# Smaller weight tiles, stores issued by ScalarE, and one threshold search in a decoder layer on one core

## The chip, the core and the metric

The kernel runs on one core of a Trainium2 chip. The core has TensorE (PE, matrix products; its weight loads are PEld), VectorE (DVE), ScalarE (ACT), GpSimd (POOL) and SyncE (SP), which here only issues DMAs. Each engine works through its own instructions in their order; semaphores hold an instruction until what it needs is done. The metric is the device time of one execution in microseconds (us).

## The reference: what is computed

One decoder layer for a sequence of 1024 tokens of width 1024, all in float32. One projection of x yields the inputs of two kinds of heads. Eight attention heads of 64 see, per query, only the 256 keys that an indexer scores highest. Four HGRN2 heads of 128 run a gated recurrence. Then come an output projection, a layer norm, an MLP and a second layer norm:

```python
proj = x @ w_in[l]
q, k, v, iq, ik, iw, hq, hf, hi, hg = jnp.split(proj, _split_points(), axis=-1)
...
score = jnp.einsum('bqh,bqhs->bqs', iwb.astype(jnp.float32), jax.nn.relu(logits))
...
_, idx = lax.top_k(score, topk)
...
mix = jnp.concatenate([att, hgo], axis=-1) @ w_o[l]
x = layer_norm(ALPHA * x + mix, ln1_g[l], ln1_b[l])
h = jnp.square(jax.nn.relu(x @ w_up[l])) @ w_down[l]
x = layer_norm(ALPHA * x + h, ln2_g[l], ln2_b[l])
```

## The kernel before

Every float32 matrix is split into a high part (rounded by ACT, line 88) and a low part (the remainder, by DVE or POOL, line 89). A product is then three matmuls (`mm3`, lines 123 to 125). For projection weights POOL makes the low part.

A tile scheduler sets the order of each engine's instructions when the kernel is built, from the program's order and modelled times. On the chip that order is fixed. Rotating buffers (`bufs`) decide how early a load can be issued: it waits until the previous user of its buffer is done.

The first 464 us, the stage that most of the change touches, are:

- 0 to 42 us: x is loaded and transposed, and the indexer's columns are projected.
- Then `turned` projects keys and queries. A pass (two PSUM banks, 48 matmuls) is followed by rope on DVE (lines 191 and 192) and POOL (193), by a split into `rparts`, and by four stores of 256 KB to DRAM (`kd`, `qd`). These DMAs are issued by SP at line 49. Between the passes stand the indexer's logits: matmuls at 282 and 283, `relu` on ACT at 286, weighted sums into six `score` tiles on DVE at 288 and 290.
- Then `natural`, `transposed` and `gates` project the recurrence's inner input (`HI`, copied by ACT at 430), its queries and gates (`hgq`, `hgf`), attention's values (`vd`, stored at line 561) and the output gates.
- Beside these stand two generators. `hgrn` is the recurrence: a unit per head, with 32x32 block products at line 482 and DVE work at 486 to 542 (`hgD` at 502 copies blocks out of PSUM). The other is the search for each query's 256th best score.

The search sets one bit of a threshold after the other, 31 in all. Four score tiles are counted by DVE (`topk_counts`): `cand` at 325 proposes a bit, four `reach` operations at 313 count scores (384 to 768 wide), `acc` at 328 and a copy at 329 keep or drop it. Two wider tiles are counted by ACT (`topk_signs`): sums of signs, `sjunk` at 345, with three small DVE operations per bit: `scand` 355, `sacc` 357, `scur` 358. `select` (381 to 388) then turns each score tile into a mask; attention's first scores, at line 691 from 464 us on, need the masks.

The weights of a projection live in `wraw` (2 buffers) and `w` (5 buffers) as tiles of two blocks of 128 rows, so that a tile of 512 columns is 512 KB to load. The table `side` says how many steps of each generator are taken beside each projection step:

Of the kernel before, what the change touches and what calls it, by code (L numbers as in the profile page):

```python
# [7 lines left out]
F32 = mybir.dt.float32  # L8
# [34 lines left out]
def layer(ctx, tc, x, w_in, w_o, lb_logits, hg_norm_g, ln1_g, ln1_b, w_up, w_down, ln2_g, ln2_b,  # L43
# [54 lines left out]
    def weight(srcs, shape, pool_every=2, after=None, halves=False, pool=None):  # L98

        raw = (pool or wp).tile([P] + shape, F32, name="wraw", tag="wraw", bufs=4 if pool else 2)  # L100
# [8 lines left out]
        w = wp.tile([P, 2] + shape, F32R, name="w", tag="w", bufs=5)  # L109
# [45 lines left out]
    def in_weights(segs, pool_every=1, pool=None):  # L155
        n = sum(b - a for a, b in segs)
        return [weight([rows(w_in, a, b, 2 * kp, 2) for a, b in segs], [2, n], pool_every, pool=pool) for kp in range(4)]

    def natural(segs, evac, ws=None):
# [3 lines left out]
        for pr in range(4):  # L163
            ps = [mm_bank((P, n)) for _ in range(2)]
            for k in range(NK):
                w = ws[k // 2]
                for i in range(2):
                    t = 2 * pr + i
                    mm3(ps[i], XH[t // 4][:, t % 4, k, :], XL[t // 4][:, t % 4, k, :],
                        w[:, 0, k % 2, :], w[:, 1, k % 2, :], k == 0, k == NK - 1)  # L170
# [4 lines left out]
    def turned(c0, dst):  # L175

        ws = [weight([rows(w_in, c0, c0 + 512, 2 * kp, 2)], [2, 512], 1, halves=True) for kp in range(4)]
        for g in range(2):
            for i in range(2):
                ps = [mm_bank() for _ in range(2)]  # L180
                for k in range(NK):
                    w = ws[k // 2]
                    for b in range(2):
                        sl = slice((2 * b + g) * P, (2 * b + g + 1) * P)
                        mm3(ps[b].rearrange("p (t n) -> p t n", t=4), w[:, 0, k % 2, sl], w[:, 1, k % 2, sl],
                            XH[i][:, :, k, :], XL[i][:, :, k, :], k == 0, k == NK - 1)
                n = slice(i * 512, (i + 1) * 512)
                for b in range(2):
# [7 lines left out]
                    for j in range(2):  # L196
                        dma(dst[j, 4 * g:4 * g + 4, b, :, n], parts[:, j].bitcast(F32))
                yield

    def transposed(segs, evac):  # L200

        ws = [weight([rows(w_in, a, b, 2 * kp, 2) for a, b in segs], [2, 512], 1) for kp in range(4)]
        for c in range(4):
            ps = [mm_bank() for _ in range(2)]
            for k in range(NK):
                w = ws[k // 2]
                sl = slice(c * P, (c + 1) * P)
                for i in range(2):
                    mm3(ps[i].rearrange("p (t n) -> p t n", t=4), w[:, 0, k % 2, sl], w[:, 1, k % 2, sl],
                        XH[i][:, :, k, :], XL[i][:, :, k, :], k == 0, k == NK - 1)  # L210
            for i in range(2):
                evac(c, i, ps[i])
# [953 lines left out]
```

## Time and profile before

| what | value |
|---|---|
| median of 3 runs | 1383.96 us (1382.64 to 1385.42) |
| the profiled execution's own time | 1383.45 us |
| its span, first to last instruction | 1381.7 us |
| mean granted TensorE clock | 0.976 of full speed |
| PE, DVE, ACT, POOL busy | 95%, 70%, 43%, 27% of the span |

The times in the trace are those of the one profiled execution. A granted clock of 1 is 2.4 GHz, of 0.5 it is 1.2 GHz, the two levels that a stretch can have; a mean between them says how much of a window ran at either. A wait is idle time of an engine, put down to the work that ended it.

### The profile page before, as it was taken

What the parts mean: (1) busy time and instruction counts of PE and PEld (TensorE: products, weight loads), DVE (VectorE), ACT (ScalarE), POOL (GpSimd) and SP (SyncE); (2) the same over time, 40 slices, a digit from 0 to 9 for tenths busy, and PEclk for the clock granted to TensorE, in tenths of its full rate; (3) what the DMA queues carried; (4) which work ended last, traced back from release to release, by engine and by line L of the source; (5) the groups of instructions that cost most, each with busy time, mean ns of one, the idle gap of its engine ahead of it and who ended that gap; (6) DMA issues with size and microseconds to landing.
All of it is one profiled execution on the core that took longest, in us unless ns stands there. A gap on an engine that the chain in (4) does not pass through costs nothing. (4 is left out here: it accounts for less than half of the span.)

```text
span 1381.7 us, 20797 instructions
## 1 busy us (share of the span) xinstructions
PE 1310.3 (95%) x7961; PEld 1067.1 (77%) x7961; DVE 968.9 (70%) x1821; ACT 594.3 (43%) x1038; POOL 371.4 (27%) x344
## 2 busy tenths in 40 slices
PE   8999799889899999999998999999998899999996
PEld 8877678677679956667887888888886688888875
DVE  4557989999993345553378755566537999887568
ACT  3333346655522455562135655555545343333131
POOL 3433302434515201132482000000003442341016
PEclk9999899999999999999999999999999999999998
DMA  5333322101103294106322544434466554443123
GB/s 219 111 101 104 101 57 61 45 20 32 48 32 92 72 192 99 36 31 199 128 99 79 176 145 160 160 130 151 154 213 240 187 196 149 157 160 92 54 100 122
DMA packets 96948, 162.50 MB, mean 118 GB/s; under 512 B 5832, under 2 KB 41040, under 8 KB 96720
## 3 DMA queue, kind: packets, MB, share of 16 engines
q1 hardware_dynamic: 81584, 133.37, 31.1%
q10 hardware_dynamic: 15264, 27.79, 5.7%
q8 instruction: 63, 1.03, 0.3%
q14 instruction: 37, 0.30, 0.1%
HBM read 114.48 MB, written 46.66 MB: 117 GB/s over the span
## 5 line engine op out<-in xcount | busy, mean ns | idle before, releaser
L123 PE MATMUL ps<-tw,sh 128*128 128x512 f32 x392 | 154.3, 396 | 8.5 <-ACT tw L88 5.1
L123 PE MATMUL ps<-w,xt 128*128 128x512 f32 (+2 forms) x448 | 158.4, 358 | 3.1 <-ACT HI L430 1.8
L125 PE MATMUL ps<-w,xt 128*128 128x512 f32 (+2 forms) x448 | 159.1, 356 | 0.0
L124 PE MATMUL ps<-w,xt 128*128 128x512 f32 (+2 forms) x448 | 158.9, 356 | 0.0
L124 PE MATMUL ps<-tw,sh 128*128 128x512 f32 x392 | 154.4, 394 | 1.5 <-DVE tw L89 1.5
L125 PE MATMUL ps<-tw,sh 128*128 128x512 f32 x392 | 153.0, 394 | 0.2 <-DVE sh L89 0.2
L89 POOL TENSOR_TENSOR w<-wraw,w 128x1024 fp32r<-128x1024 f32 (+2 forms) x46 | 95.5, 2087 | 118.5 <-ACT w L88 115.7
L1052 POOL TENSOR_TENSOR tt<-rb,rb 128x1536 f32<-128x1536 f32 (+1 forms) x5 | 19.6, 3912 | 392.1 <-DVE tw L89 314.7
L1074 DVE TENSOR_TENSOR acc<-acc,ps 128x512 f32<-128x512 f32 x140 | 92.0, 678 | 35.6 <-PE ps L125 35.5
L88 ACT ACTIVATE sh<-rs 128x1536 fp32r<-128x1536 f32 (+1 forms) x35 | 49.1, 1403 | 151.6 <-PE ps L125 141.7
L123 PE MATMUL ps<-xt,w 128*128 128x512 f32 x256 | 102.9, 402 | 0.0
L313 DVE TENSOR_SCALAR_CACHE_REDUCE junk<-score,cand 128x384 uint8<-128x384 f32 (+1 forms) x124 | 100.4, 810 | 2.7
L124 PE MATMUL ps<-xt,w 128*128 128x512 f32 x256 | 101.9, 398 | 0.0
L125 PE MATMUL ps<-xt,w 128*128 128x512 f32 x256 | 101.6, 397 | 0.0
L124 PE MATMUL ps<-xt,wq 128*128 128x512 f32 x256 | 99.9, 390 | 0.0
L123 PE MATMUL ps<-xt,wq 128*128 128x512 f32 x256 | 99.7, 390 | 0.0
L125 PE MATMUL ps<-xt,wq 128*128 128x512 f32 x256 | 99.6, 390 | 0.0
L345 ACT ACTIVATE sjunk<-score,scand 128x896 int8<-128x896 f32 (+1 forms) x62 | 67.8, 1094 | 69.5 <-DVE scand L355 53.5
L123 PEld LDWEIGHTS ps<-w,xt 128*128 128x128 f32 x448 | 86.0, 193 | 15.0 <-ACT HI L430 2.2
L124 PEld LDWEIGHTS ps<-w,xt 128*128 128x128 f32 x448 | 86.1, 192 | 11.5 <-issue 0.8
L123 PEld LDWEIGHTS ps<-tw,sh 128*128 128x128 f32 x392 | 75.0, 192 | 25.8 <-ACT tw L88 5.5
L125 PEld LDWEIGHTS ps<-w,xt 128*128 128x128 f32 x448 | 86.1, 192 | 10.4
(240 smaller groups left out, 3074.2 us busy)
## 6 DMA issues: line engine op xcount, KB each, us to landing
hs<-h ACTq DMA_DIRECT2D x98, 256.0 KB
rs<-hs SPq DMA_DIRECT2D x28, 768.0 KB
wr<-in_w_up_dram SPq DMA_DIRECT2D x16, 1024.0 KB
rb<-in_w_down_dram SPq DMA_DIRECT2D x16, 768.0 KB
wraw<-in_w_in_dram SPq DMA_DIRECT2D x20, 512.0 KB
ks<-kd SPq DMA_DIRECT2D x16, 512.0 KB
xn<-in_x_dram SPq DMA_DIRECT2D x8, 512.0 KB
kd<-rparts SPq DMA_DIRECT2D x16, 256.0 KB
```

Of the source, the lines that this page charges most:

```text
L88: first = ACT.activation(hi, src, AF.Copy)
L89: (eng or DVE).tensor_tensor(lo, src, hi.bitcast(F32), op=OP.subtract)
L123: PE.matmul(ps, ah, bh, start=first, stop=False, **kw)
L124: PE.matmul(ps, ah, bl, start=False, stop=False, **kw)
L125: PE.matmul(ps, al, bh, start=False, stop=last, **kw)
L313: DVE.tensor_scalar(junk[:, :wide[j]], score[j], at, 0.0, op0=op, op1=OP.add, accum_out=res)
L345: ACT.activation(sjunk[:, :wide[NB + j]], score[NB + j], AF.Sign, bias=0.0 if bias is None else bias[:, j:j + 1], scale=1.0, accum_out=cnt ...
L1052: POOL.tensor_tensor(t1, b12, b11, op=OP.subtract)
L1074: DVE.tensor_tensor(acc[t][:, gs], acc[t][:, gs], ps, op=OP.add)
```

## The change

Three things change, in the first stage above all.

- **Weights.** Tiles hold one block of 128 rows (two for gates) instead of two (four): eight loads of 256 KB per projection instead of four of 512 KB, with 6 instead of 2 `wraw` and 9 instead of 5 `w` buffers. The recurrence's columns load in two runs of 256 columns instead of four of 128, with the passes in the order 0, 2, 1, 3. Attention's keys (`ks`) become two tiles per head with smaller loads, and w_o has eight tiles per half.
- **Stores.** The 32 stores of keys and queries and the 8 of values are issued by ACT instead of SP.
- **One search.** `topk` counts on both engines for each bit and then uses one set of small operations over six columns; `best_keys` adds `select` for all six tiles. It is spread over the projection steps 2 to 25, where the two searches before ended at 18 and 22.

```diff
-        raw = (pool or wp).tile([P] + shape, F32, name="wraw", tag="wraw", bufs=4 if pool else 2)
+        raw = (pool or wp).tile([P] + shape, F32, name="wraw", tag="wraw", bufs=8 if pool else 6)
...
-        w = wp.tile([P, 2] + shape, F32R, name="w", tag="w", bufs=5)
+        w = wp.tile([P, 2] + shape, F32R, name="w", tag="w", bufs=9)
...
-        return [weight([rows(w_in, a, b, 2 * kp, 2) for a, b in segs], [2, n], pool_every, pool=pool) for kp in range(4)]
+        return [weight([rows(w_in, a, b, k, 1) for a, b in segs], [1, n], pool_every, pool=pool) for k in range(NK)]
...
     def turned(c0, dst):
 
-        ws = [weight([rows(w_in, c0, c0 + 512, 2 * kp, 2)], [2, 512], 1, halves=True) for kp in range(4)]
+        ws = [weight([rows(w_in, c0, c0 + 512, k, 1)], [1, 512], 1, halves=True) for k in range(NK)]
...
                     for j in range(2):
-                        dma(dst[j, 4 * g:4 * g + 4, b, :, n], parts[:, j].bitcast(F32))
+                        ACT.dma_start(dst[j, 4 * g:4 * g + 4, b, :, n], parts[:, j].bitcast(F32))
...
-    def transposed(segs, evac):
+    def transposed(segs, evac, order):
+
+        ws = [weight([rows(w_in, a, b, k, 1) for a, b in segs], [1, 512], 1) for k in range(NK)]
+        for n, c in enumerate(order):
...
-    def topk_counts():
-        cnt = tk.tile([P, NB], F32, name="cnt")
-        cand = tk.tile([P, NB], I32, name="cand")
-        acc = tk.tile([P, NB], I32, name="acc")
-        cur = thr[:, :NB].bitcast(I32)
-        for j in range(NB):
-            reach(j, 0.0, OP.is_ge, cnt[:, j:j + 1])
-        DVE.tensor_scalar(cur, cnt, float(TOPK), -1.0, op0=OP.is_lt, op1=OP.mult)
+    def topk():
+
+        n = 6 - NB
+        sjunk = tk.tile([P, S], I8, name="sjunk")
+        cnt = tk.tile([P, 6], F32, name="cnt")
+        cand = tk.tile([P, 6], I32, name="cand")
+        acc = tk.tile([P, 6], I32, name="acc")
+        need = tk.tile([P, 6], F32, name="need")
+        cur = thr.bitcast(I32)
+        turned_sign = cur[:, NB:]
+        DVE.memset(need[:, :NB], float(TOPK))
+        for j in range(NB, 6):
+            DVE.memset(need[:, j:j + 1], float(2 * TOPK - wide[j]))
+
+        def tally(at):
+            for j in range(NB, 6):
+                ACT.activation(sjunk[:, :wide[j]], score[j], AF.Sign,
+                               bias=0.0 if at is None else at[:, j:j + 1], scale=1.0, accum_out=cnt[:, j:j + 1])
+            for j in range(NB):
+                reach(j, 0.0 if at is None else at[:, j:j + 1], OP.is_ge, cnt[:, j:j + 1])
+
+        tally(None)
+        DVE.tensor_tensor(cnt, cnt, need, op=OP.is_lt)
+        DVE.tensor_scalar(cur, cnt, -1.0, None, op0=OP.mult)
+        DVE.tensor_scalar(turned_sign, turned_sign, -(1 << 31), None, op0=OP.bitwise_xor)
         yield
         for b in range(30, -1, -1):
             DVE.tensor_scalar(cand, cur, 1 << b, None, op0=OP.bitwise_xor)
-            for j in range(NB):
-                reach(j, cand[:, j:j + 1].bitcast(F32), OP.is_ge, cnt[:, j:j + 1])
-            DVE.tensor_scalar(acc, cnt, float(TOPK), None, op0=OP.is_ge)
-            DVE.copy_predicated(cur, acc, cand)
-            yield
-
-    def topk_signs():
-        n = 6 - NB
-        sjunk = tk.tile([P, S], I8, name="sjunk")
-        cnt = tk.tile([P, n], F32, name="scnt")
-        cand = tk.tile([P, n], I32, name="scand")
-        cur = tk.tile([P, n], I32, name="scur")
-        acc = tk.tile([P, n], I32, name="sacc")
-        need = tk.tile([P, n], F32, name="need")
-        for j in range(n):
-            DVE.memset(need[:, j:j + 1], float(2 * TOPK - wide[NB + j]))
-
-        def signs(bias):
-            for j in range(n):
-                ACT.activation(sjunk[:, :wide[NB + j]], score[NB + j], AF.Sign,
-                               bias=0.0 if bias is None else bias[:, j:j + 1], scale=1.0,
-                               accum_out=cnt[:, j:j + 1])
-
-        signs(None)
-        DVE.tensor_tensor(cnt, cnt, need, op=OP.is_lt)
-        DVE.tensor_scalar(cur, cnt, -1.0, None, op0=OP.mult)
-        DVE.tensor_scalar(cur, cur, -(1 << 31), None, op0=OP.bitwise_xor)
-        yield
-        for b in range(30, -1, -1):
-            DVE.tensor_scalar(cand, cur, 1 << b, None, op0=OP.bitwise_xor)
-            signs(cand.bitcast(F32))
+            tally(cand.bitcast(F32))
             DVE.tensor_tensor(acc, cnt, need, op=OP.is_ge)
             DVE.copy_predicated(cur, acc, cand)
             yield
...
-    def topk_a():
-        yield from topk_counts()
-        yield from select(range(NB))
-
-    def topk_b():
-        yield from topk_signs()
-        yield from select(range(NB, 6))
+    def best_keys():
+        yield from topk()
+        yield from select(range(6))
...
-        dma(vd[t * P:(t + 1) * P, :], r)
-
-    def gates(pair, pool, **kw):
+        ACT.dma_start(vd[t * P:(t + 1) * P, :], r)
+
...
-        ws = [weight([rows(w_in, c0, c0 + 256, 4 * kp, 4)], [4, 256], 1) for kp in range(2)]
+        ws = [weight([rows(w_in, c0, c0 + 256, 2 * kp, 2)], [2, 256], 1) for kp in range(4)]
...
-                g = pool.tile([P, 256], F32, name="gate", bufs=2, **kw)
+                g = pool.tile([P, 256], F32, name="gate", bufs=bufs, **kw)
...
-        return [(c + h * P, c + (h + 1) * P) for h in (2 * pair, 2 * pair + 1) for c in (CHQ, CHF)]
+        return [(c + 2 * pair * P, c + 2 * (pair + 1) * P) for c in (CHQ, CHF)]
...
-              13: lambda: transposed(hgrn_cols(0), hgrn_evac(0)),
-              17: lambda: transposed(hgrn_cols(1), hgrn_evac(1)),
+              13: lambda: transposed(hgrn_cols(0), hgrn_evac(0), (0, 2, 1, 3)),
+              17: lambda: transposed(hgrn_cols(1), hgrn_evac(1), (0, 2, 1, 3)),
...
-    side = [even(logits(), 0, 2, 25), even(topk_a(), 2, 18, 36), even(topk_b(), 2, 22, 38),
+    side = [even(logits(), 0, 2, 25), even(best_keys(), 2, 25, 41),
             (hgrn(), {15: 4, 16: 5, 17: 9, 18: 10, 19: 14, 20: 15, 21: 21, 22: 25}, 22)]
...
-    g1 = gates(1, wp, tag="wraw")
+    g1 = gates(1, wp, tag="wraw", bufs=6)
...
-            ks.append(wp.tile([P, 2, S], F32R, name="ks", tag="w", bufs=5))
-            for r in range(2):
-                d = dma(ks[hh][r * HD:(r + 1) * HD].bitcast(F32), kd[:, 2 * hp + hh].rearrange("j x d s -> (x d) j s"))
-                if after is not None:
-                    behind(d, after)
+            ks.append([wp.tile([P, S], F32R, name="ks", tag="w", bufs=9) for _ in range(2)])
+            for j in range(2):
+                for r in range(2):
+                    d = dma(ks[hh][j][r * HD:(r + 1) * HD].bitcast(F32), kd[j, 2 * hp + hh].rearrange("x d s -> (x d) s"))
+                    if after is not None:
+                        behind(d, after)
         va = bq.tile([P, NT, P], F32, name="va1") if hp % 2 else bp.tile([P, NT, P], F32, name="va")
...
-        ws = [weight([rows(w_o, half * 512, half * 512 + 512, 2 * kp, 2)], [2, 512], 1, after=last) for kp in range(4)]
+        ws = [weight([rows(w_o, half * 512, half * 512 + 512, k, 1)], [1, 512], 1, after=last) for k in range(NK)]
```

In the changed file `reach` is still line 313, the sign sums are line 331, `cand` 342, `acc` 344, the copy 345, the stores 197 and 543, the `HI` copy 413.

On SP, before: the rows that follow the first query stores (`qd<-rparts` is a store, `wraw<-in_w_in_dram` a weight load).

```order
L49 DMA qd<-rparts 4x32x512 [waits DMAHW5_49,DVE_49]
L49 DMA qd<-rparts 4x32x512 [waits DMAHW6_49,DVE_49]
L49 DMA wraw<-in_w_in_dram 128x2x512 [waits DMAHW7_49,Pool_49]
L49 DMA wraw<-in_w_in_dram 128x2x128 [waits DMAHW0_49,Pool_49]
...
L49 DMA wraw<-in_w_in_dram 128x2x128 x3
L49 DMA qd<-rparts 4x32x512 [waits DMAHW4_49,Activation_49]
L49 DMA qd<-rparts 4x32x512 [waits DMAHW5_49,Activation_49]
L49 DMA qd<-rparts 4x32x512 [waits DMAHW6_49,DVE_49]
```

On SP now, the place of the inner input's and the recurrence's weights:

```order
L49 DMA wraw<-in_w_in_dram 128x512 [waits DMAHW5_49,Pool_49]
L49 DMA wraw<-in_w_in_dram 128x512 [waits DMAHW7_49,DMAHW6_49,Pool_49]
L49 DMA wraw<-in_w_in_dram 128x512 [waits DMAHW6_49,DMAHW1_49,Pool_49]
L49 DMA wraw<-in_w_in_dram 128x256 [waits DMAHW2_49,DMAHW0_49,Pool_49]
L49 DMA wraw<-in_w_in_dram 128x256 [waits DMAHW1_49]
```

The stores have left SP; weight loads follow each other there. On ACT now, the last query stores and the first sign sums:

```order
L197 DMA qd<-rparts 4x32x512 [waits DMAHW1_49,DVE_49]
L286 ACTIVATE relu<-ps 128x512 [waits PE_49]
L286 ACTIVATE relu<-ps 128x512 [waits DVE_49,PE_49] x2
L413 ACTIVATE HI<-ps 128x512 [waits DMAHW6_49,DMAHW1_49,DMAHW7_49,DMAHW0_49,DVE_49]
L413 ACTIVATE HI<-ps 128x512
L331 ACTIVATE sjunk,cnt<-score_83 128x1024 [waits Pool_49]
L331 ACTIVATE sjunk,cnt<-score_82,cand 128x896 [waits DVE_49,Activation_49]
L331 ACTIVATE sjunk,cnt<-score_83,cand 128x1024 [waits Activation_49]
```

The stores now stand between the relus, and the first sign sum of the widest tile stands behind an HI copy that waits for stores (the DMAHW semaphores). On DVE before, a piece of the logits (`score` tile 82 is the fifth):

```order
L328 TENSOR_SCALAR acc<-cnt 128x4
L290 SCALAR_TENSOR_TENSOR score_82<-relu,iw,score_82 128x512
L329 COPY_PREDICATED thr<-acc,cand 128x4
L290 SCALAR_TENSOR_TENSOR score_82<-relu,iw,score_82 128x384
L325 TENSOR_SCALAR cand<-thr 128x4
L313 TENSOR_SCALAR junk,cnt<-score_78,cand 128x384
L313 TENSOR_SCALAR junk,cnt<-score_79,cand 128x512
```

On DVE now, from the last score of the last tile (83) on:

```order
L290 SCALAR_TENSOR_TENSOR score_83<-relu,iw,score_83 128x512 x4
L390 CAST level<-levelf 128x160
L337 TENSOR_TENSOR cnt<-cnt,need 128x6
L338 TENSOR_SCALAR thr<-cnt 128x6
L339 TENSOR_SCALAR thr<-thr 128x2
L342 TENSOR_SCALAR cand<-thr 128x6
L313 TENSOR_SCALAR junk,cnt<-score_78,cand 128x384
L313 TENSOR_SCALAR junk,cnt<-score_79,cand 128x512
```

The search's bits have left the logits and begin behind the last score, with one set of small operations over six columns. On PE the sequence is nearly the same: between the last matmul of the recurrence and attention's first scores stood 201 matmuls of the gates, and 125 stand there now.

## Rows read from the trace of the kernel before

**Rows 1.** The page: PE's busy time with its instructions; the chain by engine.
```profile
PE 1310.3 (95%) x7961; PEld 1067.1 (77%) x7961; DVE 968.9 (70%) x1821; ACT 594.3 (43%) x1038; POOL 371.4 (27%) x344
PE 40%; DVE 3%; issue 2%; POOL 1%; DMA 1%; ACT 0%; SPq 0%; POOLq 0%; DVEq 0%
```
**Rows 2.** Windows of all engines; after the busy times: PE clock, DMA share, GB/s.
```profile
70.00:105.00 35.00, 32.45 (x150) 26.50 (x150) 19.50 (x28) 11.55 (x24) 14.08 (x11) 1.00 0.31 101
157.00:187.00 30.00, 22.43 (x87) 17.39 (x86) 27.00 (x57) 8.75 (x14) 8.59 (x7) 0.83 0.45 125
187.00:426.00 239.00, 219.37 (x2599) 177.71 (x2598) 226.06 (x657) 120.77 (x251) 92.00 (x132) 0.96 0.16 45
426.00:464.00 38.00, 37.16 (x314) 36.96 (x313) 8.44 (x25) 8.86 (x33) 11.88 (x15) 1.00 0.31 69
```
**Rows 3.** Waits of PE, 0 to 440 us: total, times, longest.
```profile
PE ps L282 <- ACT relu L286: 11.0, 5, 4.7
PE ps L482 <- DVE hgD L502: 6.2, 5, 1.9
...
PE ps L123 <- ACT HI L430: 1.8, 1, 1.8
```
**Rows 4.** Waits of ACT, 90 to 440 us: total, times, longest.
```profile
ACT sjunk L345 <- DVE scand L355: 53.5, 21, 8.8
ACT w L88 <- DMA wraw<-in_w_in_dram: 21.8, 5, 9.0
ACT hgsq L539 <- PE ps L535: 15.8, 5, 6.5
...
ACT hgA L508 <- PE ps L482: 12.4, 6, 4.9
...
ACT HI L430 <- DMA qd<-rparts: 8.2, 1, 8.2
```
**Rows 5.** Timeline of SP's DMA issues: start us, us, and their number.
```profile
60.99 31.44 SPq L49 DMA_DIRECT2D kd<-rparts  x11
...
157.00 16.78 SPq L49 DMA_DIRECT2D wraw<-in_w_in_dram  x13
173.88 5.69 SPq L49 DMA_DIRECT2D qd<-rparts  x4
```
**Rows 6.** Windows of 5 us, columns as in the windows above.
```profile
160.00:165.00 5.00, 2.40 (x7) 1.39 (x7) 4.90 (x11) 0.29 (x1) 0.00 (x0) 0.65 0.61 194
165.00:170.00 5.00, 2.57 (x6) 2.10 (x7) 2.59 (x2) 3.36 (x5) 3.02 (x2) 0.50 0.08 24
170.00:175.00 5.00, 5.00 (x19) 4.02 (x19) 4.93 (x6) 1.10 (x3) 4.82 (x3) 0.83 0.82 201
```
**Rows 7.** The tile rparts, 118 to 192 us: issue ns min/median/max, first and last start.
```profile
L49 SPq DMA_DIRECT2D qd<-rparts x16: 502/508/584, 121.7 to 179.1; - x16
```
**Rows 8.** Windows of line 328 alone (acc, once per bit): DVE busy, count.
```profile
122.00:187.00 65.00, 2.11 (x6) 0.92 0.34 104
```
**Rows 9.** Timeline of DVE: the acc operations of two bits that follow each other.
```profile
201.79 0.17 DVE L328 TENSOR_SCALAR acc<-cnt 128x4 int32<-128x4 f32 x1
...
205.83 0.17 DVE L328 TENSOR_SCALAR acc<-cnt 128x4 int32<-128x4 f32 x1
```
**Rows 10.** Groups of DVE by line and shape, 42 to 440 us: busy, mean ns.
```profile
L357 DVE TENSOR_TENSOR sacc<-scnt,need 128x2 int32<-128x2 f32 x31 | 10.6, 341 | 1.3 <-ACT sjunk L345 1.2
...
L358 DVE COPY_PREDICATED scur<-sacc,scand 128x2 int32<-128x2 int32 x31 | 10.2, 329 | 0.0
...
L355 DVE TENSOR_SCALAR scand<-scur 128x2 int32<-128x2 int32 x31 | 9.7, 312 | 0.0
```
**Rows 11.** The page's group of the sign sums (two per bit): busy, mean ns.
```profile
L345 ACT ACTIVATE sjunk<-score,scand 128x896 int8<-128x896 f32 (+1 forms) x62 | 67.8, 1094 | 69.5 <-DVE scand L355 53.5
```
**Rows 12.** Waits of PE, 440 to 560 us: total, times, longest.
```profile
PE ps L691 <- DMA ks<-kd: 2.9, 1, 2.9
```
**Rows 13.** Timeline of SP's DMA issues, 478 to 505 us: start us, us, number.
```profile
489.41 2.52 SPq L49 DMA_DIRECT2D ks<-kd  x4
```

More of the change, by code (lines that the diff above doesn't have):

```diff
@@ L165, in natural @@
             for k in range(NK):
-                w = ws[k // 2]
+                w = ws[k]
                 for i in range(2):
@@ L169, in natural @@
                     mm3(ps[i], XH[t // 4][:, t % 4, k, :], XL[t // 4][:, t % 4, k, :],
-                        w[:, 0, k % 2, :], w[:, 1, k % 2, :], k == 0, k == NK - 1)
+                        w[:, 0, 0, :], w[:, 1, 0, :], k == 0, k == NK - 1)
             for i in range(2):
@@ L181, in turned @@
                 for k in range(NK):
-                    w = ws[k // 2]
+                    w = ws[k]
                     for b in range(2):
                         sl = slice((2 * b + g) * P, (2 * b + g + 1) * P)
-                        mm3(ps[b].rearrange("p (t n) -> p t n", t=4), w[:, 0, k % 2, sl], w[:, 1, k % 2, sl],
+                        mm3(ps[b].rearrange("p (t n) -> p t n", t=4), w[:, 0, 0, sl], w[:, 1, 0, sl],
                             XH[i][:, :, k, :], XL[i][:, :, k, :], k == 0, k == NK - 1)
@@ L196, in turned @@
                     for j in range(2):
-                        dma(dst[j, 4 * g:4 * g + 4, b, :, n], parts[:, j].bitcast(F32))
+                        ACT.dma_start(dst[j, 4 * g:4 * g + 4, b, :, n], parts[:, j].bitcast(F32))
                 yield
-    def transposed(segs, evac):
-        ws = [weight([rows(w_in, a, b, 2 * kp, 2) for a, b in segs], [2, 512], 1) for kp in range(4)]
-        for c in range(4):
+    def transposed(segs, evac, order):
+        ws = [weight([rows(w_in, a, b, k, 1) for a, b in segs], [1, 512], 1) for k in range(NK)]
+        for n, c in enumerate(order):
             ps = [mm_bank() for _ in range(2)]
             for k in range(NK):
-                w = ws[k // 2]
+                w = ws[k]
                 sl = slice(c * P, (c + 1) * P)
                 for i in range(2):
-                    mm3(ps[i].rearrange("p (t n) -> p t n", t=4), w[:, 0, k % 2, sl], w[:, 1, k % 2, sl],
+                    mm3(ps[i].rearrange("p (t n) -> p t n", t=4), w[:, 0, 0, sl], w[:, 1, 0, sl],
                         XH[i][:, :, k, :], XL[i][:, :, k, :], k == 0, k == NK - 1)
             for i in range(2):
-                evac(c, i, ps[i])
+                evac(n, i, ps[i])
             yield
@@ L359, in topk_signs @@
             yield
+        DVE.tensor_scalar(turned_sign, turned_sign, -(1 << 31), None, op0=OP.bitwise_xor)
         t = thr[:, NB:]
-        DVE.tensor_scalar(t.bitcast(I32), cur, -(1 << 31), None, op0=OP.bitwise_xor)
         least = tk.tile([P, n], F32, name="least")
@@ L372, in topk_signs @@
             yield
-        DVE.tensor_scalar(acc, cnt, float(TOPK), None, op0=OP.is_ge)
-        DVE.copy_predicated(t, acc, least)
+        DVE.tensor_scalar(acc[:, :n], cnt[:, :n], float(TOPK), None, op0=OP.is_ge)
+        DVE.copy_predicated(t, acc[:, :n], least)
         yield
@@ L559, in v_evac, with gates @@
         ACT.activation(r, ps, AF.Copy)
-        dma(vd[t * P:(t + 1) * P, :], r)
-    def gates(pair, pool, **kw):
+        ACT.dma_start(vd[t * P:(t + 1) * P, :], r)
+    def gates(pair, pool, bufs=2, **kw):
         c0 = CHG + 256 * pair
-        ws = [weight([rows(w_in, c0, c0 + 256, 4 * kp, 4)], [4, 256], 1) for kp in range(2)]
+        ws = [weight([rows(w_in, c0, c0 + 256, 2 * kp, 2)], [2, 256], 1) for kp in range(4)]
         for q in range(4):
@@ L568, in gates @@
             for k in range(NK):
-                w = ws[k // 4]
+                w = ws[k // 2]
                 for i in range(2):
@@ L690, in scores @@
                 ps = mm_bank()
-                PE.matmul(ps[:, :n], qs[:, hh, t * P:(t + 1) * P], ks[hh][:, 0, c], start=True, stop=False)
-                PE.matmul(ps[:, :n], qs[:, hh, t * P:(t + 1) * P], ks[hh][:, 1, c], start=False, stop=True)
+                PE.matmul(ps[:, :n], qs[:, hh, t * P:(t + 1) * P], ks[hh][0][:, c], start=True, stop=False)
+                PE.matmul(ps[:, :n], qs[:, hh, t * P:(t + 1) * P], ks[hh][1][:, c], start=False, stop=True)
                 DVE.tensor_tensor_reduce(pr[hh][:, c], ps[:, :n], mask[:, c], 1.0, mx[:, 0, hh:hh + 1] if ci else -HUGE,
@@ L886, in layer @@
                     mm3(ps[i], MH[t // 4][:, t % 4, k, :], ML[t // 4][:, t % 4, k, :],
-                        ws[k // 2][:, 0, k % 2, :], ws[k // 2][:, 1, k % 2, :], k == 0, k == 3)
+                        ws[k][:, 0, 0, :], ws[k][:, 1, 0, :], k == 0, k == 3)
             for i in range(2):
```

2 lines of the change are left out of this document (1 added, 1 removed).

## The prediction

> **What bounds the kernel now.** I read the page first. PE is busy in 1310.3 us of the span and its matmuls are the chain that ended last; no other engine has more than 3% of that chain [rows 1]. So the change can gain only where PE waits or runs at the lower clock, and lose only where it makes PE wait. Then I cut the stretch that the change touches into windows at events of the kernel [rows 2]. From 70 to 105 us (keys and logits) PE is busy 32.45 of 35; from 157 to 187 (last queries, last logits) 22.43 of 30 at a granted clock of 0.83; from 187 to 426 (inner inputs, recurrence, search) 219.37 of 239 at 0.96, while DVE is busy 226.06, the fullest engine there; from 426 to attention's first scores at 464 PE is busy 37.16 of 38 and DVE only 8.44. PE's waits up to 440 us name two kinds of releaser [rows 3]: ACT's relu of the logits (11.0 us in 5 waits) and ACT's HI copy (1.8), and DVE's recurrence operations, hgD first (6.2). The reader should see two limits: before 187 us ACT is late, after it DVE is full.
>
> Why ACT is late in the first part: it waited 21.8 us in 5 waits for weights (the longest 9.0), and 8.2 us, before its first HI copy, for stored queries to land [rows 4]. ACT issues neither. SP does, one after the other [rows 5]: 11 key stores hold it from 60.99 for 31.44 us, since each waits for its half to be computed, and the weight load that ACT wants stands behind them. From 157.00 on, 13 weight loads that wait for buffers hold SP for 16.78 us, and the last four query stores are issued only at 173.88. PE's waits cost more than themselves: from 160 to 170 us PE was busy 4.97 of 10 us, at granted clocks of 0.65 and 0.50 [rows 6], the lower of its two levels for most of it.
>
> **The change, part by part.** The sum is made against the profiled execution's own 1383.45 us, 0.5 below the median of the runs.
>
> *Stores on ACT's queue, finer ring.* Removed: weight loads no longer stand behind key and query stores on SP, nor the last stores behind weight loads. Upper bound of the gain: the relu waits 11.0, the HI wait 1.8, and the lower clock. A mean of 0.65, 0.50 and 0.83 is the lower level for 70, 100 and 34% of a slice; work there takes double, so of 2.40, 2.57 and 5.00 us busy 0.8, 1.3 and 0.8 are lost, 3 in all. Together 16. Lower bound: nothing, if relus become late for a new reason. There is one: ACT now issues 32 key and query stores and 8 value stores. On SP one took 0.51 us [rows 7], so 40 of them are 20 us of ACT's queue, 16 of these before 187. The store of the lower half also waits for DVE, with relus and weight splits queued behind it. ACT is busy only 11.55 of 35 us there [rows 2], so most of this fits, not all. I take -11, nearer the upper bound: the inner inputs, the last score and the search's start come near 176 instead of 187.
>
> The Trainium skill ("DMA: Bandwidth & Descriptors", section "Issuing engines are not separate DMA queues") says that SP's and ACT's queues are served by the same DMA engines, so a second issuer brings no bandwidth. By that rule, if bandwidth were what delays the weights, this term would be nothing. The row speaks for the other reading: the DMA share is 0.31 from 70 to 105 us [rows 2], so the order of issue made the weights late.
>
> *One search loop.* Two effects on DVE, of opposite sign. Against it: before, the four-tile count search started among the logits and had done 6 of its 31 bits, and most of the next, by 187 us [rows 8]. Now all stand behind the last score. An undisturbed bit took 4.04 us (from 201.79 to 205.83 [rows 9]), so 6.5 bits put 26 us of work into the stretch where DVE is full. For it: three small operations per bit go, sacc, scur and scand, 10.6 + 10.2 + 9.7 = 30.5 us of busy time [rows 10]. Where such operations overlap, as in an undisturbed bit, each starts about 0.1 us after the last, so three cost 0.3 and 31 bits 10. Between 10 and 30 I take 20. In all, DVE gets 6 us more work between the last score and attention's first scores.
>
> The order changes where this work stands. I counted it on both orders and priced every operation at its line's mean in the stretch from 187 us on (657 records, 226 us busy [rows 2]). From the last score to the first recurrence operation it is 64 us before and 55 after; to the last unit's last hgD, 219 and 207; to attention's first scores, 230 and 236. The reason: most selection operations now stand late, among the last unit's work, so that the added work fills the time after 426, where DVE idled. DVE thus reaches recurrence work 9 to 12 us sooner, plus the 11 from the earlier start, less what ACT costs the loop.
>
> That last cost is new: acc now waits for ACT's sign sums in every bit, and behind acc stands everything on DVE, recurrence included. A pair of sign sums is twice 1.09 us [rows 11] plus reads of the accumulator; the counts of the same bit, 4.04 less the small operations, over 3. So a pair fits, but not a pair behind an ACT instruction that waits for PE. Such waits were 15.8 (hgsq) and 12.4 us (hgA) [rows 4], harmless so far since the sign search had 53.5 us of slack [rows 4]. Bounds: nothing, and these 28 us passed on whole. I take 3 to the first unit and 6 to the last, since in most bits recurrence operations of DVE cover ACT's waits.
>
> So DVE's lead is 9 + 11 - 3 = 17 us at the first unit and 12 + 11 - 6 = 17 at the last. PE's own work from 187 to 426 is 219 less 9 for the lower clock (a mean of 0.96 is the lower level for 8% of the time, and half of that is lost), 210 of 239 us, so PE could gain 29 more; DVE still sets the end. For the whole stretch to 464 I take DVE's lead: **-17**, the first part's 11 included. The tail can follow: the last unit's last output matmuls now stand 76 gate matmuls further back in PE's order, so DVE's later end costs no wait.
>
> *Attention's fetch.* PE waits 2.9 us for keys of the second head pair, issued at 489.41 behind w_o, queries and values [rows 12, 13]. With six small buffers four of the w_o loads can be issued while the gates run, so less stands ahead of the keys. At least 0; at most twice 2.9, if the clock falls after this wait as it did in [rows 6]. I take **-3**.
>
> *The rest.* Eight index loads instead of four at the start: at 0.51 us per issue, 0 to +2; I take **+1**. POOL's splits in smaller pieces and w_o's tiles lie beside a busy PE: nothing; with that cover gone, weights would come late by a piece's split.
>
> Sum: -17 - 3 + 1 = -19, so 1383.45 - 19 = 1364.5, against the median **1365**.
>
> **Rivals.**
> *ACT holds the search (slower).* Sign sums stand behind ACT instructions that wait for PE, which waits for DVE, which waits for the sign sums. For it: the 28 us above, in the very stretch where DVE is full. Against it: DVE work between the bits. At 1 us per bit, 31 in all and 25 more than I took, the lead of 17 becomes 8 us behind: 1365 + 25 = **1390**. It decides from about 0.8 us per bit on, where 6 + 19 are lost.
> *The stores only move the wait.* ACT loses in store issues and their waits most of what it gains in weights: the first part gives 2 instead of 11, the lead shrinks to 8, **1374**. For it: 20 us of issues; against it: ACT's small load.
> *Nothing comes of it.* The small operations save only 10 (10 us less lead) and the first part gives 2: the lead is gone, the fetch's 3 and the start's 1 remain: **1382**.
> *DVE stops being the limit.* The small operations save 30, the loop waits for nothing, and the fetch gives 6: 17 + 10 + 6 + 3 = 36 less at most, half of the added part likelier: **1354**, at best 1348.
>
> Within 0.2% (2.8 us) a measurement of this kernel tells nothing from no change.
>
> **How the numbers follow.** The forecast with its own range of 1358 to 1373 has 0.47, moved waits (to 1380) 0.15, nothing 0.08, DVE no limit 0.13, ACT holds the search 0.17. So faster 0.75, same 0.08, slower 0.17. For 8 in 10 I leave out the far end of the fast case and the upper half of the slow one: 1350 to 1389.
>
> **What the changed profile would show.** PE's waits for relu fall from 11.0 to 4 us or less and ACT's for weights under 8: right on the stores. The first recurrence operation comes about 17 us earlier, and DVE is still over 94% busy from there to the last unit: right on the order. DVE's acc waits for sjunk 10 us or less in all: right on the coupling; 25 or more, and the slow rival holds. Attention's first scores start near 447 instead of 464. The forecast would be wrong if ACT's HI copy still waits long for stores to land, since the first sign sum stands behind it, or if PE's waits for DVE in the recurrence stay as they are.

## The result

The changed kernel takes 1360.01 us (median of 4, 1358.40 to 1361.02) against 1383.30 for the kernel before in the same session. The ratio is 0.9831, 95% interval 0.9810 to 0.9852: faster by 23 us, where 19 were forecast. The profiled execution took 1360.71 us; its span is 1358.5.

The windows of the changed kernel, cut near the same events as [rows 2]: 143 to 168 us are the last queries and logits, 174 lies just before the first HI copy (175.29), 441 just before attention's first scores (443.0, against 463.7 in the kernel before).

```profile
70.00:105.00 35.00, 35.00 (x165) 29.06 (x163) 27.66 (x34) 14.25 (x28) 20.96 (x16) 1.00 0.40 125
143.00:168.00 25.00, 23.86 (x103) 18.80 (x102) 12.75 (x15) 11.43 (x21) 12.77 (x10) 1.00 0.46 146
168.00:174.00 6.00, 6.00 (x28) 4.92 (x28) 1.00 (x2) 0.00 (x0) 1.23 (x3) 1.00 0.38 137
174.00:405.00 231.00, 216.09 (x2593) 175.98 (x2592) 218.97 (x608) 124.56 (x269) 92.15 (x147) 0.97 0.15 42
405.00:441.00 36.00, 35.33 (x301) 34.96 (x300) 28.67 (x49) 7.39 (x29) 13.45 (x14) 1.00 0.34 78
```

The first part has lost its stalls: PE is full from 70 to 105 us, and the granted clock no longer falls before 168 us. DVE is still full in the long stretch, and the window before attention, where it was busy 8.44 of 38 us, is now filled too. PE's waits up to 440 us, answering to [rows 3]:

```profile
PE ps L465 <- DVE hgD L485: 7.9, 7, 2.3
...
PE ps L465 <- DVE hgk L483: 4.4, 2, 3.9
PE ps L516 <- DVE hgst L511: 2.2, 4, 0.7
PE ps L282 <- ACT relu L286: 1.1, 2, 1.0
```

The relu waits fell from 11.0 to 1.1 us and the HI wait is gone; the waits for the recurrence's DVE work stayed. On ACT, answering to [rows 4], waits before weight splits fell from 21.8 to 1.8 us, but the HI copy still waited 7.3 us for stored queries, and the sign sums have as much slack as before:

```profile
ACT sjunk L331 <- DVE cand L342: 62.8, 26, 5.5
...
ACT HI L413 <- DMA qd<-rparts: 7.3, 1, 7.3
...
ACT w L88 <- DMA wraw<-in_w_in_dram: 1.8, 2, 1.5
```

For attention's keys PE now waits 0.8 and 0.7 us, where it waited 2.9 [rows 12]:

```profile
PE ps L676 <- DMA ks<-kd: 0.8, 1, 0.8
PE ps L675 <- DMA ks<-kd: 0.7, 1, 0.7
```

**Where the time came from.** All kernels here run the same 7961 matmuls in nearly the same sequence. So I summed the streamed columns of PE's matmuls in order of start and asked, for a moment of the kernel before, how much earlier another kernel has streamed as many. The table has that lead, in us, worked out from the traces at five moments of the kernel before: 200 (inner inputs), 410 (late in the recurrence), 463 (attention's first scores), 510 (behind the fetch of the second pair) and 1300. Runs e1 to e12 are the experiments below. Each row is one execution, and the runs of one kernel differ by 2 to 6 us: e7 and e8, whose first part is that of the changed kernel, read 15.8 and 15.4 at 200 instead of 16.7, so a difference of 1 us tells nothing. The profiled execution of e8 and of e9 was the slowest of its kernel, that of e12 the fastest.

| kernel | profiled us | 200 | 410 | 463 | 510 | 1300 |
|---|---|---|---|---|---|---|
| changed | 1360.71 | 16.7 | 27.7 | 20.7 | 24.4 | 23.7 |
| e4: ring alone | 1364.64 | 10.8 | 16.0 | 17.9 | 21.2 | 19.2 |
| e6: stores alone | 1374.18 | 9.1 | 15.6 | 6.0 | 9.3 | 8.9 |
| e9: search alone | 1380.44 | 4.2 | 11.5 | 4.8 | 3.6 | 3.6 |
| e2: ring and stores | 1370.05 | 12.4 | 14.4 | 11.7 | 15.8 | 14.9 |
| e1: ring and search | 1365.09 | 12.7 | 18.9 | 15.1 | 19.6 | 18.8 |
| e3: stores and search | 1373.79 | 6.7 | 17.4 | 11.0 | 9.2 | 9.6 |
| e5: changed, 4 raw buffers | 1360.54 | 14.8 | 24.9 | 17.9 | 23.3 | 24.2 |
| e10: changed, old columns | 1366.19 | 11.3 | 26.8 | 19.5 | 19.8 | 17.8 |
| e7: changed, all selections late | 1367.23 | 15.8 | 25.5 | 27.4 | 21.4 | 18.1 |
| e8: changed, four selections late | 1365.68 | 15.4 | 26.3 | 22.7 | 20.3 | 19.5 |
| e11: changed, signs first | 1359.07 | 16.2 | 33.4 | 25.1 | 26.7 | 25.5 |
| e12: e11 with four selections late | 1359.68 | 16.9 | 34.1 | 27.1 | 25.7 | 24.6 |

The changed kernel gained 16.7 us in the first part and 11 more by 410, gave 7.0 back before attention, and gained 3.7 in the fetch.

### The profile page after: what moved, and what is told of

It reads as the page before. It is cut to its first block, busy times and chain, and to the rows that moved or that the text cites. A ratio compares the mean times of both kernels' runs of the same rounds, so it can differ in the third digit from the quotient of the medians.

```text
span 1358.5 us, 20928 instructions
## 1 busy us (share of the span) xinstructions
PE 1303.1 (96%) x7961; PEld 1062.0 (78%) x7961; DVE 960.3 (71%) x1730; ACT 599.1 (44%) x1070; POOL 378.4 (28%) x374
## 4 chain that ended last, share of the span: by engine, by line
PE 69%; DVE 17%; DMA 5%; POOL 4%; issue 3%; ACT 1%; SPq 0%; DVEq 0%; POOLq 0%; ACTq 0%
PE ps L123 19%; PE ps L124 19%; PE ps L125 19%; DVE junk L313 6%; PE ps L720 3%; PE ps L694 2%; DVE hgk L483 1%; PE ps L675 1%; DVE hgq L482 1%; POOL tn L895 1%; PE ps L676 1%; DMA kd<-rparts 1%; DMA rb<-in_w_down_dram 1%; POOL acc L821 1%; DMA va<-vd 1%
## 5 line engine op out<-in xcount | busy, mean ns | idle before, releaser
L89 POOL TENSOR_TENSOR w<-wraw,w 128x512 fp32r<-128x512 f32 (+1 forms) x76 | 102.3, 1367 | 105.4 <-ACT w L88 69.7
L331 ACT ACTIVATE sjunk<-score,cand 128x896 int8<-128x896 f32 (+1 forms) x62 | 67.9, 1095 | 65.4 <-DVE cand L342 62.8
```

The lines of the kernel that those rows point to most:

```text
L89: (eng or DVE).tensor_tensor(lo, src, hi.bitcast(F32), op=OP.subtract)
L331: ACT.activation(sjunk[:, :wide[j]], score[j], AF.Sign, bias=0.0 if at is None else at[:, j:j + 1], scale=1.0, accum_out=cnt[:, j:j + 1])
```

## The experiments

### Which of the three parts it was (e1 to e4, e6, e9)

Each part was taken out of the changed kernel, and each put alone into the kernel before.

e1 puts the stores back on SP:

```diff
-                        ACT.dma_start(dst[j, 4 * g:4 * g + 4, b, :, n], parts[:, j].bitcast(F32))
+                        dma(dst[j, 4 * g:4 * g + 4, b, :, n], parts[:, j].bitcast(F32))
...
-        ACT.dma_start(vd[t * P:(t + 1) * P, :], r)
+        dma(vd[t * P:(t + 1) * P, :], r)
```

> The changed kernel with the 40 stores of keys, queries and values issued by SP again; ring and single search kept. Theory A (order of issue on SP made the weights late): the first part's gain of 13 to 15 us at the start of the inner inputs is lost, 1372 us (1368 to 1376), ACT again waits for weights over 10 us. Theory B (the finer ring freed the weights, whoever issues the stores): at most 1363 us.

1364.93 us, ratio 0.9875 (0.9850 to 0.9900). Neither theory: A lost, since only 4 of the first part's 16.7 us went, and B was a little too sharp.

e2 brings back the two searches (`topk_counts`, `topk_signs`, `topk_a`, `topk_b` as in the diff's minus lines):

```diff
-    side = [even(logits(), 0, 2, 25), even(best_keys(), 2, 25, 41),
+    side = [even(logits(), 0, 2, 25), even(topk_a(), 2, 18, 36), even(topk_b(), 2, 22, 38),
```

> The changed kernel with the two separate searches of before; ring and stores as changed. Theory A (the single loop gives DVE a lead of about 10 us in the recurrence): the first part's gain stays but the recurrence gives back some of it, 1368 us (1364 to 1372). Theory B (the saved small operations only pay for the bits that moved behind the logits, so the loop is worth nothing): 1358 to 1362 us.

1369.36 us, 0.9897 (0.9868 to 0.9926), the time that A gave. But of the 9 us against the changed kernel 4.3 were lost in the first part already, where I had expected none, and from 200 to 463 the lead falls by only 0.7 us where it grows by 4.0 in the changed kernel.

e3 is the kernel before with the stores on ACT and the single search, on its old ring:

```diff
-        raw = (pool or wp).tile([P] + shape, F32, name="wraw", tag="wraw", bufs=8 if pool else 6)
+        raw = (pool or wp).tile([P] + shape, F32, name="wraw", tag="wraw", bufs=4 if pool else 2)
...
-        ws = [weight([rows(w_in, c0, c0 + 512, k, 1)], [1, 512], 1, halves=True) for k in range(NK)]
+        ws = [weight([rows(w_in, c0, c0 + 512, 2 * kp, 2)], [2, 512], 1, halves=True) for kp in range(4)]
```

> The kernel before with stores on ACT and the single search, but its old ring of large weight tiles, its old column runs and its old key tiles. Theory A (the ring is worth only the attention fetch): 1364 us (1361 to 1367), PE again waits about 3 us for the second pair's keys, the first part as in the changed kernel. Theory B (the finer ring is what brings the weights in time): 1370 us or more, with ACT waiting for weights over 10 us.

1373.91 us, 0.9938 (0.9914 to 0.9961): theory B. ACT again waited for weights, though no store stood on SP:

```profile
ACT w L88 <- DMA wraw<-in_w_in_dram: 20.9, 6, 6.8
```

e4 is the opposite: the ring alone, stores on SP, two searches (the diff's weight hunks and no other).

> The kernel before with the ring of single tiles (with its column runs and key tiles) alone; stores on SP, two searches. Theory A: only the fetch's gain, 1379 us (1376 to 1382). Theory B (the ring brings the weights): 1372 us or less, PE's waits for relu under 5 us.

1364.23 us, 0.9872 (0.9845 to 0.9899). Theory B, and the largest part of the whole gain: 19 of 23 us from the ring alone. The tile `wraw` from 60 to 190 us, in the kernel before and then in e4 (duration ns min/median/max, first and last start):

```profile
L89 POOL TENSOR_TENSOR w<-wraw,w x11: 1255/1735/2563, 90.3 to 169.3; 128x512 fp32r<-128x512 f32 x6, 128x1024 fp32r<-128x1024 f32 x5
```

```profile
L89 POOL TENSOR_TENSOR w<-wraw,w x16: 1275/1334/1760, 88.1 to 161.0; 128x512 fp32r<-128x512 f32 x16
```

SP is still held by stores there, from 116.34 for 30.14 us:

```profile
116.34 30.14 SPq L49 DMA_DIRECT2D qd<-rparts  x11
```

So the order of issue was not what made the weights late, at least not most of it. SP and POOL in the kernel before, from 91 us on, show what did:

```profile
90.84 1.59 SPq L49 DMA_DIRECT2D kd<-rparts  x2
93.69 0.38 SPq L49 DMA_DIRECT2D wraw<-in_w_in_dram  x1
```

```profile
91.93 1.73 POOL L89 TENSOR_TENSOR w<-wraw,w 128x512 fp32r<-128x512 f32 x1
```

The stores have left SP at 92.43 us, but the weight load goes out at 93.69, when POOL has split the second half of the tile whose buffer it takes (91.93 + 1.73 = 93.66). In e4 the first such load goes out at 89.42, after one split that ended at 89.38. A smaller piece gives its buffer back after one split instead of two, and its own split is shorter: POOL's takes up to 1.76 us instead of 2.56, and the last split of this stretch starts at 161.0 instead of 169.3. PE's waits for relu fell from 11.0 to 4.0 us. Why the ring alone loses none of this lead in the recurrence, while e6 (below) does, no run here shows.

e6 moves the stores alone, e1's edit the other way round on the kernel before.

> The kernel before with the 40 stores issued by ACT and nothing else. Theory A (the order of issue on SP costs the first part most of its 16 us): 1373 us or less. Theory C (after the first runs: with large tiles the buffers, not SP's order, make weights late, and the search among the logits keeps ACT and DVE late): 1378 to 1385 us, with ACT still waiting for weights near 20 us.

1375.35 us, 0.9938 (0.9915 to 0.9961), between the two. The first part gained 9.1 us, the end of the recurrence gave back 9.6 (15.6 at 410, 6.0 at 463), and ACT waited 16.4 us for weights.

e9 puts the single search alone into the kernel before.

> The kernel before with the single search and nothing else. Theory (from the runs so far: the single loop is worth something only where stores on ACT leave the logits to a free DVE; with stores on SP it neither gains nor loses): 1380 to 1386 us. Rival (its saved operations and its order gain by themselves, as the prediction had it): 1375 us or less. Third: the moved bits make it slower, 1388 us or more.

1376.93 us, 0.9953 (0.9935 to 0.9971): a gain, though none was expected. Its row of the table, from its slowest execution, is low.

| | two searches | one search |
|---|---|---|
| old ring, stores on SP | 1383.30 | 1376.93 |
| old ring, stores on ACT | 1375.35 | 1373.91 |
| new ring, stores on SP | 1364.23 | 1364.93 |
| new ring, stores on ACT | 1369.36 | 1360.01 |

The single gains, 19.1 + 8.0 + 6.4 = 33 us, are not a sum: the parts remove the same waits, so together they give 23. On the new ring stores and search pay only together: the search alone is worth nothing there (1364.93 against 1364.23), and with two searches the stores on ACT are rather worse (1369.36, though the intervals of the two ratios overlap). The 4 to 5 us that both bring together are near the limit of what is told apart: the interval of the changed kernel overlaps those of e1 and e4 at its edge, though its slowest run is faster than the fastest of either.

### What in the ring (e5, e10)

e5 has as many bytes of raw buffers as the kernel before, in smaller pieces:

```diff
-        raw = (pool or wp).tile([P] + shape, F32, name="wraw", tag="wraw", bufs=8 if pool else 6)
+        raw = (pool or wp).tile([P] + shape, F32, name="wraw", tag="wraw", bufs=8 if pool else 4)
...
-    g1 = gates(1, wp, tag="wraw", bufs=6)
+    g1 = gates(1, wp, tag="wraw", bufs=4)
```

> The changed kernel with 4 instead of 6 buffers for loaded weight tiles, as many bytes as the two large ones of before. Theory G (the finer grain of the ring is what helps: a buffer comes free and a split can start after 256 KB): 1362 us (1359 to 1365). Theory D (it is the deeper look-ahead of six buffers): 1368 us or more, the first part's lead at the inner inputs back near 7 us.

1361.09 us, 0.9835 (0.9806 to 0.9864), not told apart from the changed kernel. So it is the grain, not more bytes of look-ahead.

e10 restores the recurrence's column runs and, with them, the order of the passes:

```diff
-        return [(c + 2 * pair * P, c + 2 * (pair + 1) * P) for c in (CHQ, CHF)]
+        return [(c + h * P, c + (h + 1) * P) for h in (2 * pair, 2 * pair + 1) for c in (CHQ, CHF)]
...
-              13: lambda: transposed(hgrn_cols(0), hgrn_evac(0), (0, 2, 1, 3)),
+              13: lambda: transposed(hgrn_cols(0), hgrn_evac(0), (0, 1, 2, 3)),
```

> The changed kernel with the recurrence's columns loaded in four runs of 128 again, passes in the order 0 to 3. Theory (the grain of the tiles, not the runs, makes the ring's gain): 1359 to 1363 us. Rival (the short rows of the old runs hold the queue and the engines): 1366 us or more, with ACT waiting for these weights after 170 us.

1364.46 us, 0.9860 (0.9836 to 0.9884): between the theories; the interval overlaps that of the changed kernel at its edge. The trace shows a loss in the first part. From 160 to 165 us PE is busy 1.92 of 5 us, in the changed kernel (second row) 4.84:

```profile
160.00:165.00 5.00, 1.92 (x7) 1.24 (x6) 1.52 (x3) 1.38 (x3) 0.07 (x1) 0.79 0.68 132
```

```profile
160.00:165.00 5.00, 4.84 (x22) 3.63 (x21) 1.43 (x3) 0.60 (x1) 0.00 (x0) 1.00 0.51 159
```

PE waits 3.1 us there for a relu, and ACT 3.9 us before that relu for a weight load; later relus stand behind query stores and wait 6.0 us until 171. At a DMA share of 0.68 no more is moved (132 GB/s, in the changed kernel 159 at a share of 0.51). That fits short rows that keep the DMA engines busy. But there are also more loads to issue: from 101 to 172 us SP issues 31, where the changed kernel has 22 from 93 to 161, and no run here separates the two or the order of the passes. So up to 4 us of what the ring brings may belong to the columns and not to the grain.

### Why the lead was given back before attention (e7, e8, e11, e12)

In the changed kernel PE waits 3.9 us at 396 us. DVE's timeline there:

```profile
394.50 1.25 DVE L361 COPY_PREDICATED thr<-acc,least 128x2 f32<-128x2 int32 x1
395.68 0.74 DVE L374 SCALAR_TENSOR_TENSOR score<-score,thr,equal 128x512 f32<-128x512 f32 x1
396.34 1.13 DVE L313 TENSOR_SCALAR_CACHE_REDUCE junk<-score,thr 128x896 uint8<-128x896 f32 x1
...
397.76 1.54 DVE L370 TENSOR_SCALAR equal<-score,thr 128x640 f16<-128x640 f32 x1
399.22 0.41 DVE L482 TENSOR_TENSOR hgq<-hgq,hgt 128x256 f32<-128x256 f32 x1
```

Selections stand ahead of the last unit's hgq and hgk. The granted clock falls behind this wait: it is 0.66 from 400 to 405 us. e7 makes all of them wait:

```diff
-            reach(j, thr[:, j:j + 1], OP.is_gt, rest[:, j:j + 1])
+            d = reach(j, thr[:, j:j + 1], OP.is_gt, rest[:, j:j + 1])
+            if j >= 0:
+                behind(d, tail[0])
...
-            DVE.tensor_tensor(kv[:, :, 0, :], kv[:, :, 0, :], t2[:, :, 1:2].to_broadcast([P, nb, m]), op=OP.mult)
+            tail[:] = [DVE.tensor_tensor(kv[:, :, 0, :], kv[:, :, 0, :], t2[:, :, 1:2].to_broadcast([P, nb, m]), op=OP.mult)]
```

> The changed kernel, with the selection of all six tiles made to wait for the last unit's last scaling of hgk, so that no selection stands among that unit's DVE work before it. Theory (the tail gives back about 5 us because selections hold DVE before the last unit's products): PE's wait of 3.9 us at 396 us goes, 1355 us (1353 to 1358). Rival (DVE's total up to attention's first scores decides, the order within it does not): 1359 to 1362 us, and slower if masks come late.

1366.89 us, 0.9871 (0.9842 to 0.9900). The wait at 396 us went, as the theory said: the lead is 27.4 us at 463 instead of 20.7. Then 11 us were lost at attention's start, down to 16.0 at 470. The chain of waits shows how:

```profile
438.11 1.34 DVE score L376
439.47 5.12 DMA qs<-qd
444.59 2.70 issue
447.29 0.45 PE ps L678
```

The load of attention's queries (`qs`) is issued when the last selection's operation on the scores is done: SP waited for it.

```profile
SPq L49 <- DVE score L376: 14.7, 1, 14.7
```

PE waits 4.3 us before the first score; the load lands in that time, at 444.59, and the profile names nothing for the last 2.7. It waits 4.1 us before that for the last unit's output, whose gates stand among the same selections on DVE, and the granted clock is 0.50 from 443 to 450 us. The changed kernel has the same order without the wait, since its selections end earlier: the last such operation ends at 429.54 us (first row), and the load goes out at 429.57.

```profile
427.90 1.64 DVE L374 SCALAR_TENSOR_TENSOR score<-score,thr,equal 128x1024 f32<-128x1024 f32 x1
```

```profile
429.57 1.28 SPq L49 DMA_DIRECT2D qs<-qd  x2
```

So the end of the selections, not the masks as such, gates attention through this load. That it waits because its tile reuses memory of the selection's temporaries is an inference from the code (`es_t` closes before attention's pools open); no run here moved that memory.

e8 delays only the tiles 2 to 5 (`j >= 2`).

> As the run before, but only the selections of the tiles 2 to 5 wait. Same theory: 1356 us (1354 to 1358); rival: 1359 to 1362 us.

1362.21 us, 0.9836 (0.9805 to 0.9868): the rival. PE waits 2.4 us for the same load, and the lead falls from 22.7 at 463 to 17.1 at 470, of which the fetch returns 3.2.

e11 starts the search earlier instead. In the changed kernel DVE is nearly idle from 168 to 174 us (1.00 of 6 us, the windows above), because the first sign sum stands on ACT behind the HI copy that waits for stores:

```diff
     def hi_evac(t, ps):
-        ACT.activation(HI[:, t, :], ps, AF.Copy)
+        d = ACT.activation(HI[:, t, :], ps, AF.Copy)
+        if t < 8:
+            behind(d, signs[3])
```

(`signs` collects the sign sums; the fourth is the last of the first bit.)

> The changed kernel, with all HI copies made to wait for the sign sums of the search's first bit, so that these no longer stand behind the HI copy that waits 7.3 us for stored queries. Theory (from the last score on, DVE's total work sets when the recurrence and attention come, so an earlier start is kept): the search starts near 169 instead of 176 us, the first recurrence operation comes some 5 us earlier, 1355 us (1353 to 1358). Rival (PE's own order or the masks set the end, or PE waits for late HI copies): 1359 to 1362 us.

1359.08 us, 0.9822 (0.9803 to 0.9841), the rival's time, not told apart from the changed kernel. The theory's first half shows in the trace: DVE is busy 3.16 of 6 us where it was 1.00, the first recurrence operation comes 4.6 us earlier, and the lead at 410 grows from 27.7 to 33.4:

```profile
168.00:174.00 6.00, 6.00 (x28) 4.92 (x28) 3.16 (x10) 2.74 (x5) 1.23 (x3) 1.00 0.41 145
```

Then 8.3 us are given back before 463 (PE waits 5.2 us for hgst behind selections), and the fetch returns 1.6 instead of 3.7.

e12 joins e11 and e8.

> The changed kernel with the first bit's sign sums ahead of the HI copies (as in the run before) and the selections of the tiles 2 to 5 behind the last unit's last scaling of hgk (as in an earlier run). Theory (the earlier start leaves DVE some 5 us before attention, so the selections can stand late without holding attention): the wait near 382 us shrinks to 2 us or less, attention does not wait, 1356 us (1353 to 1358). Rival (DVE's total up to attention decides, whatever its order): the wait only moves to attention's start, 1359 to 1363 us.

1363.12 us, 0.9858 (0.9839 to 0.9876): the rival. In its profiled execution, its fastest, PE waits 4.2 us for hgst and 4.3 at attention's start for the queries:

```profile
PE ps L523 <- DVE hgst L518: 4.8, 2, 4.2
PE ps L682 <- DMA qs<-qd: 4.3, 1, 4.3
```

No version tried here beats the changed kernel beyond its interval.

## Why the prediction was right, and where its steps were not

The time, the sign and the mechanism of "late weights, then a full DVE" held. That the total came within 5 us of the forecast is in part luck: the lead late in the recurrence was larger than forecast and 7 us of it were lost again. Both signs that the prediction had named for being wrong came, too: the HI copy still waited 7.3 us for stores (8.2 before), and PE's waits for hgD rose from 6.2 to 7.9 us, with 4.4 for hgk. Step by step:

*Stores and finer ring, -11.* The two together measured 12.4 us (e2 at 200): the term was right as a sum. Its reason was not. The prediction blamed the order of issue on SP, and read the weight load behind the key stores as held by them; it was held last by its buffer (93.69, above). The order alone (e6) gives 9.1 us there, the ring alone (e4), with the same order on SP, gives 10.8 and keeps it, while e6 loses it late in the recurrence. The ring was costed as a part of this term and of the fetch; it is the one part that brings most of the 23 us by itself. ACT's cost of an issue was sized well: a store takes 0.53 us there, close to the 0.51 on SP [rows 7].

*The rule of the Trainium skill* ("DMA: Bandwidth & Descriptors", section "Issuing engines are not separate DMA queues") warned that a second issuer brings no bandwidth. No run here measures that. The times fit it on the new ring with two searches, where moving the stores to ACT gained nothing (1369.36 against 1364.23); on the old ring it gained 8 us (1375.35 against 1383.30), so there it did change which work stands behind the stores.

*The single search: 26 us of moved bits against.* The step counted moving the bits as a cost only. It also freed the logits: with both other parts in place the first part gained another 4.3 us from it (16.7 against 12.4), and the last score comes at 168.0 us, where it comes at 175.6 in e2 and at 185.7 in the kernel before. The likely reason, that DVE's scores and halves no longer stand among counts, was not tested by itself.

*The small operations, -20.* This term was too large. Added up, their durations fell by 30.7 us (the six of before, of which [rows 10] shows three, had 55.8 in all, the three now have 25.1), but such operations overlap others. DVE's busy time between the last score and attention's first scores rose by 13 us instead of 6 (below), so that they saved about 13, an estimate from these 13 and the 26 of the moved bits. An undisturbed bit is no shorter at all, 4.05 us here against 4.04 [rows 9]:

```profile
181.75 0.17 DVE L344 TENSOR_TENSOR acc<-cnt,need 128x6 int32<-128x6 f32 x1
...
185.80 0.17 DVE L344 TENSOR_TENSOR acc<-cnt,need 128x6 int32<-128x6 f32 x1
```

The three start one after the other, 0.20 to 0.21 us apart, each from the result of the last, where those of before, from two searches, started 0.08 to 0.20 us apart (237.06 to 237.58 us). The saving may lie in the bits that run beside POOL (last section); no run here measured it by itself.

*ACT's coupling, 3 to 6 us.* In the bits it measured nothing: in DVE's waits from 174 us on no acc waits for a sign sum. Only the search's start did, once, behind the late HI copy:

```profile
DVE cnt L337 <- ACT sjunk L331: 5.8, 1, 5.8
```

*DVE's lead of 17 sets the end.* DVE's first recurrence operation came at 236.6 instead of 256.8 us, 20 earlier, and the lead late in the recurrence was 27.7, larger than forecast: no coupling in the bits, more gained in the first part. Of the 9 us that the new order was to save up to there, fewer than 3 are seen (67.8 us from the end of the last score on, against 70.3), since DVE stood nearly idle for 8.7 us before the first bit. Here the slow rival was far off.

*"The tail can follow, so DVE's later end costs no wait."* This step failed. 7 us of the lead were given back between 410 and 463: the selections among the last unit's work delay its hgq and hgk, and in e7 delaying them instead delayed attention's queries. The new order is not needed for such a loss: e6, with the two searches, gives back 9.6 us there, with PE waiting 3.3 and 2.9 us for DVE, and selections stand among the last unit's operations there, too. DVE was busy 218.97 + 28.67 = 248 us from 174 us to attention, where it had been 226.06 + 8.44 = 235 [rows 2]: 13 us more, not 6. The larger lead and this loss cancel to 20.7 where 17 were forecast.

*Fetch, -3:* 3.7, the size that was forecast. The reason, six small buffers, is not needed for it: e5 with four gains 5.4 us there. Even e6, on the old ring, gains 3.3: it waits 2.1 us instead of 2.9, and its granted clock stays at 1.00, where that of the kernel before is 0.50 from 504 to 508 us. *Start, +1:* nothing that can be told (the lead is +0.5 us at 40 us, and from -1.6 to +0.3 in the other runs). *The rest, nothing:* the lead falls by 1.4 us behind the fetch (24.4 at 510, 23.0 at 650). Every run with six buffers loses 1.3 to 1.6 us there, e5 with four and tiles as fine 0.2, the old rings of e3, e6 and e9 none: so it goes with the six buffers and not with the tiles, and how stays open.

## What to carry to other kernels

When a load is split by two engines before PE can use it, look at which wait ends last before the load is issued; here it was the buffer, and halving the piece brought more than deeper buffers or another issuer. Edits that remove the same wait do not add up: measure each alone and each left out. Where an engine is full over a long stretch, work that is moved later in its order has to end somewhere; look for the load or buffer that waits for its last instruction.

## What had not been expected of the hardware

Two of the search's small DVE operations took the time of a split when POOL was splitting beside them. In the changed kernel POOL runs four splits in a row, and the copy and the next cand, 0.17 us each in the undisturbed bit at 182 us, take 1.21 us each:

```profile
195.72 5.03 POOL L89 TENSOR_TENSOR w<-wraw,w 128x512 fp32r<-128x512 f32 x4
```

```profile
198.12 0.17 DVE L344 TENSOR_TENSOR acc<-cnt,need 128x6 int32<-128x6 f32 x1
198.32 1.21 DVE L345 COPY_PREDICATED thr<-acc,cand 128x6 int32<-128x6 int32 x1
199.57 1.21 DVE L342 TENSOR_SCALAR cand<-thr 128x6 int32<-128x6 int32 x1
200.82 0.61 DVE L313 TENSOR_SCALAR_CACHE_REDUCE junk<-score,cand 128x384 uint8<-128x384 f32 x1
```

The count behind them keeps its 0.61 us. The Trainium skill ("SBUF — State Buffer", section "🔬 SBUF: two separate sides") describes a port pair that DVE and POOL hold in turn for a whole instruction; the trace agrees in the size of the wait, one split of about 1.26 us (5.03 / 4).
